# S5 read-out products put off behind the next query product, with banks from the heads' pool, in a hybrid decoder layer in fp32

## The chip, the cores and the metric

The kernel runs on one core of a Trainium2 chip, in one launch. The metric is device time in microseconds (us); the median of three runs stands for a kernel. Five engines work side by side, each through its own list of instructions in order: TensorE (PE, matmuls, with its weight loads as PEld), VectorE (DVE), ScalarE (ACT), GpSimd (POOL) and SyncE (SP, which issues most DMAs).

## The reference, cut to what matters

One layer is computed for 16 meta tokens and 2048 prompt tokens, and for one step of 8 decoding streams. A norm and one input projection feed two mixers. The S5 mixer (A) runs a complex diagonal state over the tokens for 32 groups of 16 channels, reads it out and puts it through gelu and a gate. The HGRN mixer (B) has 4 heads with a 128x128 state each. Both go through an output projection, and then comes a gated ConvFFN.

```python
u, q, fl, iv, g = columns of rms_norm(h) @ w_in
# A: S5
x  = einsum(u, bb)                       # input into 64 complex states a group
h  = associative_scan(a, x)              # h_t = a h_{t-1} + x_t
y  = Re(einsum(h, c)) + d * u
y  = gelu(y);  y5 = y * sigmoid(y @ w_glu + b_glu)
# B: HGRN2, per head, in chunks
f  = lb + (1 - lb) * sigmoid(fl);  k = 1 - f
o  = qd @ S + mask(qd @ kd^T) @ v;  S = f_chunk * S + kd'^T @ v
yh = rms_norm(o) * norm_g * silu(g)
h  = h + concat(y5, yh) @ w_out
h  = h + (silu(conv(a)) * v) @ w_down    # a, v = rms_norm(h) @ w_up
```

## The kernel before

All large products are in fp32, done as three passes on fp32r halves: high by high, low by high, high by low. Activations lie as pairs `ah`, `al`, weights as `wh` (made by ACT, L449) and `wl` (by DVE, L83). Tokens go in four blocks of 512; block 0 also carries the 16 meta tokens and the 8 streams as extra columns.

**Heads.** In each block `head()` runs four times. It makes the forget-gate product f (L480, 24 matmuls of 512 columns), its tanh (L642), the scans and the reciprocal on DVE (L645 to L665), the query product q (L480, 24 more), and the input and gate product i/g (L500, 96 matmuls of 256 columns, in two halves `t2_`). Then comes the attention part: kd by qd (L723) and the transposes of kd (L729) into two banks, the masked copy att (L726), kd by v (L734) into a third bank, the output (L746, L747), its norm and the gate (L756). Its last step, the transposes into feature order (L768), is a closure in the list `PEND`.

**S5.** The S5 work of block b-1 runs in the heads of block b. It has eight table steps `bt` of four groups each. `s5()` takes two steps before each head in blocks 1 and 2. In the last block it takes four steps of block 2 before each of heads 0 and 1; before head 2 it runs the first four steps of the last block itself, between the halves of the output projection of block 2, and two steps before each of heads 2 and 3. A step loads its table (L881, `big`, two buffers), makes the input products Bk (L896, four fp32 matmuls), swaps real and imaginary halves on ACT (L272, L273), multiplies and scans on DVE (L86, L80, L934), swaps and multiplies back (L86, L83) to the state G (`sA`), and then reads out: six products with the direct term (L945) and G (L948) into one bank, which ACT copies to Y (L954). For the S5 work of block 0 six more small products (L960, L963) read out the extra columns. Every second step ends in `s5_finish()`: gelu on DVE with one tanh on ACT (L851 to L856), four transposes of Y (L863; L872 for the extra columns), the high half by ACT (L866) and the low half by DVE (L867). The finish is a closure in `PEND`, too.

**Order.** A scheduler fixes the order of each engine's instructions when the kernel is built; what stands in a row on PE runs in that row. Buffers of a pool are given out in the order of the program, and a tile gets its buffer only when the last user of the one before it is through. PSUM has eight banks in three pools: `bank()` (3, `mm`) for large products, `tbank()` (2, `tp`) for Bk, read-outs and transposes, and `gbank()` (3, `hg`) for the attention banks L723, L729 and L734 and the transposes L768. `flush()` runs what is in `PEND`. It stands in `head()` behind the f product, in `u_proj()` behind each of its four products, in `stage_out()` and at the end of the mixers.

Of the kernel before, what the change touches and what calls it, by code (L numbers as in the profile page):

```python
# [9 lines left out]
F32 = mybir.dt.float32  # L10
F32R = mybir.dt.float32r
U32 = mybir.dt.uint32
AF = mybir.ActivationFunctionType
# [24 lines left out]
def kernel(  # L38
# [468 lines left out]
    def tm_wide(src, c0, lhs, done, ex=None, first=None, rows=None):  # L507


        pb = [(bank, gbank)[t % 2]() for t in range(4)]  # L510
        pe = bank() if ex is not None else None
        for i in range(4):
            wu = first if first is not None and i == 0 else w_unit(src, 2 * i, 2, c0, 512)
            if i == 1:
                rows()
            for t in range(4):
                for kk in range(2):
                    k = 2 * i + kk
                    for j, (wi, ai) in enumerate(PASS):
                        mm(pb[t], lhs(ai, k, t), wu[wi][:, kk, :], start=(k == 0 and j == 0),  # L520
                           stop=(k == 7 and j == 2))
                if i == 3:
                    done(t, pb[t])
            if ex is not None:
                stat, m = ex
                for kk in range(2):
                    for j in range(2):
                        mm(pe[:m], stat[:, 2 * i + kk, :m], wu[j][:, kk, :], start=(i + kk + j == 0),
                           stop=(i == 3 and kk == 1 and j == 1))
        return pe  # L530
# [96 lines left out]
    PEND = []  # L627

    def flush():
        while PEND:  # L630
            PEND.pop(0)()


    def head(b, a, h):
# [8 lines left out]
        flush()  # L643
# [23 lines left out]
        pq = fm_mm(wq, a, 8, cols)  # L667
        qd = P
# [148 lines left out]
    def u_proj(b, a):  # L817
# [60 lines left out]
    def s5(b, ut, m, bts, later=None):  # L878
        for bt in bts:
            tab = bigt()  # L880
# [22 lines left out]
            if b == 0:  # L903
# [4 lines left out]
                mw = sm.tile([128, 4, 4], F32, name="mw", bufs=1)  # L908
# [18 lines left out]
                he = sm.tile([128, 4, 9], F32, name="he", bufs=1)  # L927
# [14 lines left out]
            py = v3(tbank(), 4, 64)  # L942
            o = None
            for i in range(2):
                behind(mm(py[:, 2 * i:2 * i + 2, :].rearrange("p a b -> p (a b)"), UT[:, i, 0:128], T[:, i, :],  # L945
                          start=True, stop=False), o)
                for j in range(2):
                    o = mm(py[:, 2 * i:2 * i + 2, :].rearrange("p a b -> p (a b)"), G[:, 2 * i + j, 0:128],  # L948
                           Cm[:, 2 * i + j, :], start=False, stop=(j == 1))
            half = bt % 2  # L950
            if half == 0:
                Y = E["Y"] = s5p.tile([128, 4, 128], F32, name="sY")
            Y = E["Y"]
            ACT(Y[:, :, 64 * half:64 * half + 64].rearrange("p t (g c) -> p g t c", c=16),  # L954
                py.rearrange("p g (t c) -> p g t c", c=16), AF.Copy)
            if b == 0:
                pye = v3(tbank(), 4, 64)
                o = None
                for i in range(2):
                    behind(mm(pye[:9, 2 * i:2 * i + 2, :].rearrange("p a b -> p (a b)"),  # L960
                              UT[:, i, 131:140], T[:, i, :], start=True, stop=False), o)
                    for j in range(2):
                        o = mm(pye[:9, 2 * i:2 * i + 2, :].rearrange("p a b -> p (a b)"), he[:, 2 * i + j, :],  # L963
                               Cm[:, 2 * i + j, :], start=False, stop=(j == 1))
                if half == 0:
                    E["ye"] = s5p.tile([128, 4, 128], F32, name="sY")
                ye = E["ye"]
                ACT(ye[:9, :, 64 * half:64 * half + 64].rearrange("p t (g c) -> p g t c", c=16),
                    pye[:9].rearrange("p g (t c) -> p g t c", c=16), AF.Copy)
            if half == 1:  # L970
                fin = lambda m, bt=bt, Y=Y, ye=E.get("ye"): s5_finish(b, bt, Y, ye, m)
                if later is None:
                    PEND.append(lambda fin=fin: fin(m))
                else:
                    later.append(fin)
# [173 lines left out]
    flush()  # L1149
# [208 lines left out]
```

## Time and profile before

| | us |
|---|---|
| median of 3 runs | 2537.81 |
| lowest and highest run | 2536.32, 2539.64 |
| the profiled execution | 2535.7 |
| its span in the trace | 2534.0 |
| PE busy in the span | 2445.5 |
| DVE busy in the span | 1453.3 |
| ACT busy in the span | 902.6 |

The trace comes from the profiled execution. Its span leaves out what lies around the program, 1.7 us here. A busy time is the sum of an engine's work over the whole span, so it averages over stages: norms, set-up, tables and block 0 first; then blocks 1 to 3 with the S5 work, whose read-outs (L945) start between 276.7 and 952.1 us; and the FFN, which fills the window from 1060 to 2500 us. A matmul in three passes shows as three rows; an fp32 matmul (L723, L896, L945, L948, L863) shows as two passes, so that a row with x8 holds four of them. Matmul ends overlap the next start.

### The profile page before, as it was taken

The page shows a single profiled execution, that of the slowest core. Times are in us where ns is not written, and L with a number is a line of the kernel's source. Part 1 is how long each engine was busy: PE and PEld are TensorE (multiplying, and loading weights), DVE is VectorE, ACT ScalarE, POOL GpSimd, SP SyncE. Part 2 cuts the span into 40 slices and gives each one's busy share as a digit, 9 for nine tenths or more (in the row PEclk, how much of TensorE's full clock was granted, in tenths as well). Part 3 has the DMA queues.
Part 4 walks back from the last instruction along what each step waited for, and adds up shares of the span by engine and source line. Part 5 has one row for each costly group of instructions (what it writes and reads, how often), then busy time and mean ns, then how long its engine had stood idle before and what let it go on. Part 6 is the DMA issues. An engine that isn't in the chain of part 4 may idle for free.

```text
span 2534.0 us, 33854 instructions
## 1 busy us (share of the span) xinstructions
PE 2445.5 (97%) x13515; PEld 2088.5 (82%) x13515; DVE 1453.3 (57%) x2950; ACT 902.6 (36%) x1548; POOL 166.6 (7%) x252
## 2 busy tenths in 40 slices
PE   7989899999999989999999999999999999999998
PEld 6878787788888778888989898988788888888886
DVE  6897788688678688553343434445843433343344
ACT  3554445344435444432313131323531313131222
POOL 2223001000100001000000000000400000000000
PEclk9999999999999999999999999999999999999999
DMA  4357435543564555531111111111621111111112
GB/s 126 103 159 205 114 101 141 191 142 127 148 215 158 162 164 192 170 92 43 50 44 48 47 45 42 46 55 59 211 66 50 44 48 50 50 50 50 34 54 80
DMA packets 251260, 252.13 MB, mean 99 GB/s; under 512 B 11303, under 2 KB 208751, under 8 KB 246998
## 3 DMA queue, kind: packets, MB, share of 16 engines
q1 hardware_dynamic: 241088, 220.42, 28.8%
q0 software_dynamic: 9840, 29.48, 3.6%
q8 instruction: 106, 1.74, 0.3%
q14 instruction: 52, 0.43, 0.1%
q10 hardware_dynamic: 174, 0.06, 0.0%
HBM read 216.41 MB, written 33.27 MB: 99 GB/s over the span
## 4 chain that ended last, share of the span: by engine, by line
PE 72%; DVE 11%; issue 4%; ACT 3%; DMA 1%; POOL 1%; SPq 0%; POOLq 0%; ACTq 0%; DVEq 0%
PE mm L480 42%; PE mm L1282 9%; PE hg L1282 9%; PE mm L500 3%; PE hg L520 3%; PE mm L520 2%; DVE sB L86 2%; DVE sA L934 1%; DVE wl L83 1%; DVE sA L86 1%; PE mm L539 1%; DVE hf L665 1%; POOL rstd L546 1%; DMA x<-h_d 1%; PE tp L572 1%
## 5 line engine op out<-in xcount | busy, mean ns | idle before, releaser
L480 PE MATMUL mm<-ah,wh 128*128 128x512 f32 (+3 forms) x2312 | 811.6, 351 | 5.9 <-ACT ah L577 3.3
L480 PE MATMUL mm<-al,wh 128*128 128x512 f32 (+3 forms) x2312 | 810.8, 351 | 1.1 <-DVE al L83 1.1
L480 PE MATMUL mm<-ah,wl 128*128 128x512 f32 (+3 forms) x2312 | 810.8, 351 | 1.0 <-DVE wl L83 1.0
L449 ACT ACTIVATE wh<-st 128x1024 fp32r<-128x1024 f32 (+1 forms) x264 | 276.4, 1047 | 709.2 <-PE mm L480 298.0
L83 DVE TENSOR_TENSOR wl<-st,wh 128x1024 fp32r<-128x1024 f32 (+1 forms) x264 | 318.4, 1206 | 350.4 <-ACT wh L449 348.4
L480 PEld LDWEIGHTS mm<-ah,wh 128*128 128x128 f32 x2312 | 438.9, 190 | 59.7 <-ACT ah L577 3.9
L480 PEld LDWEIGHTS mm<-ah,wl 128*128 128x128 f32 x2312 | 438.7, 190 | 56.2 <-issue 1.6
L480 PEld LDWEIGHTS mm<-al,wh 128*128 128x128 f32 x2312 | 438.1, 189 | 54.8 <-DVE al L83 1.6
L86 DVE TENSOR_TENSOR c<-c,mm 128x512 f32<-128x512 f32 (+1 forms) x110 | 63.6, 580 | 211.7 <-PE mm L480 210.3
L500 PE MATMUL mm<-wh,ah 128*128 128x256 f32 x512 | 146.3, 286 | 3.0 <-DVE hP L86 1.7
L500 PE MATMUL mm<-wl,ah 128*128 128x256 f32 x512 | 144.8, 284 | 1.7 <-DVE wl L83 1.7
L500 PE MATMUL mm<-wh,al 128*128 128x256 f32 x512 | 145.9, 285 | 0.0
L1282 PE MATMUL mm<-wh,gh 128*128 128x512 f32 x352 | 137.4, 390 | 0.0
L1282 PE MATMUL hg<-wh,gl 128*128 128x512 f32 x352 | 137.1, 390 | 0.0
L1282 PE MATMUL hg<-wl,gh 128*128 128x512 f32 x352 | 137.1, 390 | 0.0
L1282 PE MATMUL mm<-wh,gl 128*128 128x512 f32 x352 | 137.1, 389 | 0.0
L1282 PE MATMUL mm<-wl,gh 128*128 128x512 f32 x352 | 137.1, 389 | 0.0
L1282 PE MATMUL hg<-wh,gh 128*128 128x512 f32 x352 | 137.0, 389 | 0.0
L80 DVE TENSOR_TENSOR hacc<-hacc,hg 128x512 f32<-128x512 f32 x96 | 65.8, 686 | 88.2 <-PE hg L1282 87.7
L1220 ACT ACTIVATE c<-c 128x512 f32<-128x512 f32 x88 | 55.6, 632 | 144.8 <-DVE c L1219 144.8
L80 DVE TENSOR_TENSOR hacc<-hacc,mm 128x512 f32<-128x512 f32 x96 | 65.7, 685 | 66.0 <-PE mm L1282 65.8
L500 PEld LDWEIGHTS mm<-wh,ah 128*128 128x128 f32 x512 | 97.7, 191 | 4.7 <-DVE hP L86 2.5
(406 smaller groups left out, 3569.0 us busy)
## 6 DMA issues: line engine op xcount, KB each, us to landing
st<-in_ffn_w_up_dram SPq DMA_DIRECT2D x96, 512.0 KB, 3.8
big<-tab_d SPq DMA_DIRECT2D x32, 1156.0 KB, 5.4
st<-in_w_in_dram SPq DMA_DIRECT2D x48, 512.0 KB, 5.0
st<-in_ffn_w_down_dram SPq DMA_DIRECT2D x40, 512.0 KB, 3.5
st<-in_w_in_dram SPq DMA_DIRECT2D x64, 256.0 KB, 3.1
st<-in_w_out_dram SPq DMA_DIRECT2D x32, 512.0 KB, 3.6
x<-in_x_prompt_dram SPq DMA_DIRECT2D x30, 512.0 KB, 5.0
h_d<-x POOLq DMA_DIRECT2D x16, 512.0 KB, 4.2
```

What stands on the lines that cost most here:

```text
L80: tt_(o, a, b, op=OP.add)
L83: tt_(o, a, b, op=OP.subtract)
L86: tt_(o, a, b, op=OP.mult)
L449: ACT(hi[:, :n], st[:, :n], AF.Copy)
L480: mm(p[:, :n], w[wi][:, k, :], a[ai][:, k, c0:c0 + n], start=(i == 0), stop=(i == 3 * nk - 1))
L500: o = mm(dst, lhs(ai, k), (hi, lo)[wi][:, kk, :], start=(i == 0), stop=(i == tot - 1))
L520: mm(pb[t], lhs(ai, k, t), wu[wi][:, kk, :], start=(k == 0 and j == 0), stop=(k == 7 and j == 2))
L539: mm(dst[:m], stat[:, k, :m], w[:, kk, :], start=(i == 0), stop=(i == tot - 1))
L546: nc.gpsimd.tensor_tensor(r, r, mhalf[:ss.shape[0], :n], op=OP.pow)
L572: nc.tensor.transpose(p[:, k, :], x[:, kk * 128:kk * 128 + 128], ident)
L1220: ACT(c, c, AF.Silu)
L1282: mm(ps_[t], gs[b, f0 + k][ai][:, t * 128:t * 128 + 128], wus[i][wi][:, kk, :], start=(k == 0 and j == 0), stop=(k == nf - 1 and j == 2))
```

## The change

The read-out products of a step (L945, L948, and L960, L963 for the extra columns), the copies to Y and the hand-over to `s5_finish` become a closure `products`, put into `PEND`; `s5()` runs the list itself if two closures of its call are waiting. Their banks, and those of the transposes in `s5_finish`, come from `gbank()`. In `head()`, `flush()` moves from behind the tanh of f to behind the q product, and it is called in `tm_wide()` with the second weight tile. The finish goes to a second list, `PEND2`, which `flush2()` runs (after `flush()`) behind each half of the i/g products, behind the products 1 to 3 of `u_proj()`, in `stage_out()` and at the end. Two small tiles of the extra columns change: `mw` gets another shape, `he` a second buffer.

```diff
@@ tm_wide
                 if i == 3:
                     done(t, pb[t])
+            if i == 1:
+                flush()
@@
-    PEND = []
+    PEND, PEND2 = [], []
...
+    def flush2():
+        flush()
+        while PEND2:
+            PEND2.pop(0)()
@@ head
             ACT(f[:, q0:q0 + n], p[:, :n], AF.Tanh, scale=0.5)
-        flush()
...
         pq = fm_mm(wq, a, 8, cols)
+        flush()
...
             ACT(g[:, 2 * t2_:2 * t2_ + 2], p[:, :, 128:256], AF.Silu)
+            flush2()
@@ u_proj
-            flush()
+            (flush if ch == 0 else flush2)()
@@ s5_finish
-        p = v3(tbank(), 4, 128)
+        p = v3(gbank(), 4, 128)
...
-            p = v3(tbank(), 3, 16)
+            p = v3(gbank(), 3, 16)
@@ s5
+        backs = []
         for bt in bts:
+            if len(backs) > 1:
+                flush()
+                backs.clear()
...
-                mw = sm.tile([128, 4, 4], F32, name="mw", bufs=1)
+                mw = v3(sm.tile([128, 40], F32, name="mw", bufs=1), 4, 4)
...
-                he = sm.tile([128, 4, 9], F32, name="he", bufs=1)
+                he = sm.tile([128, 4, 9], F32, name="he", bufs=2)
...
-            py = v3(tbank(), 4, 64)
-            o = None
-            for i in range(2):
...
+            def products(bt=bt, UT=UT, T=T, G=G, Cm=Cm, he=he if b == 0 else None):
+                py = v3(gbank(), 4, 64)
+                o = None
+                for i in range(2):
...
-                pye = v3(tbank(), 4, 64)
...
+                    pye = v3(gbank(), 4, 64)
...
-                    PEND.append(lambda fin=fin: fin(m))
+                        PEND2.append(lambda: fin(m))
...
+            backs.append(products)
+            PEND.append(products)
@@ stage_out
-        flush()
+        flush2()
@@ behind the last block
-    flush()
+    flush2()
```

The rows below are PE's order at two places, first before and then after. In the rows of after the lines have moved: L908 is Bk (L896 before), L959 and L962 are the products (L945, L948), L974 and L977 those of the extra columns, L871 and L880 the transposes (L863, L872), L731 and L737 attention's first two (L723, L729), L742 kd by v (L734), L754 and L755 the output (L746, L747). Names: `hg`, `tp` and `mm` are banks of the three pools, `U` the S5 input, `sA` G, `sY` Y, `big` a table, `hk`, `hP`, `hv`, `hf` the head's kd, qd, v and transposed kd.

On PE in block 1, the end of head 0 before: the last i/g product, attention, and the first f products of head 1.

```order
L500 MATMUL mm<-wl,ah 128x256
L723 MATMUL hg<-hP,hk 128x128 x4
L729 MATMUL hg<-ident,hk 128x128 x4
L746 MATMUL mm<-hv,att 128x128
L747 MATMUL mm<-Sp,hP 128x128
L734 MATMUL hg<-hv,hf 128x128 x4
L746 MATMUL mm<-hv,att 128x128
L480 MATMUL mm<-ah,wh 128x512
```

Thirty rows on in the same list, amid the f products of head 1, stand head 0's transposes and the first S5 work of the block.

```order
L480 MATMUL mm<-ah,wl 128x512
L768 MATMUL hg<-ident,hg 128x128 x4
L896 MATMUL tp<-U,big 128x148 x4
L480 MATMUL mm<-ah,wh 128x512
L480 MATMUL mm<-al,wh 128x512
L945 MATMUL tp<-big,U 128x128
L500 MATMUL mm<-wh,ah 128x256
```

The same place after, from the last products of the pair's second step on; the Bk products of both steps and the other products stand directly ahead of these rows, and ahead of those the last i/g product of head 0.

```order
L962 MATMUL hg<-big,sA 128x128 x2
L959 MATMUL hg<-big,U 128x128
L962 MATMUL hg<-big,sA 128x128 x2
L908 MATMUL tp<-U,big 128x148 x4
L871 MATMUL hg<-ident,sY 128x128 x4
L880 MATMUL hg<-ident,sY 128x9 x3
L731 MATMUL hg<-hP,hk 128x128 x4
L737 MATMUL hg<-ident,hk 128x128 x4
L908 MATMUL tp<-U,big 128x148 x3
L742 MATMUL hg<-hv,hf 128x128 x4
L754 MATMUL mm<-hv,att 128x128
L755 MATMUL mm<-Sp,hP 128x128
```

The first pair's Bk products, products and transposes have moved from amid head 1's products to between head 0's i/g products and its attention.

On PE in the last block, the end of head 1 before: the last i/g products, attention, a Bk product, and a read-out.

```order
L500 MATMUL mm<-wh,al 128x256
L500 MATMUL mm<-wl,ah 128x256
L723 MATMUL hg<-hP,hk 128x128 x4
L729 MATMUL hg<-ident,hk 128x128 x4
L896 MATMUL tp<-U,big 128x128 x4
L734 MATMUL hg<-hv,hf 128x128 x4
L746 MATMUL mm<-hv,att 128x128
L747 MATMUL mm<-Sp,hP 128x128
L948 MATMUL tp<-big,sA 128x128 x2
L945 MATMUL tp<-big,U 128x128
L948 MATMUL tp<-big,sA 128x128 x2
```

Further on in the list of before, amid the L480 of the projection that follows, stand the last but one transposes and the last read-out (the last transposes come 26 rows behind these).

```order
L480 MATMUL mm<-al,wh 128x512
L863 MATMUL tp<-ident,sY 128x128 x4
L948 MATMUL tp<-big,sA 128x128 x2
L945 MATMUL tp<-big,U 128x128
L948 MATMUL tp<-big,sA 128x128 x2
L480 MATMUL mm<-ah,wl 128x512
```

The end of head 1 after.

```order
L500 MATMUL mm<-wl,ah 128x256
L871 MATMUL hg<-ident,sY 128x128 x4
L962 MATMUL hg<-big,sA 128x128 x2
L959 MATMUL hg<-big,U 128x128
L962 MATMUL hg<-big,sA 128x128 x2
L871 MATMUL hg<-ident,sY 128x128 x4
L731 MATMUL hg<-hP,hk 128x128 x4
L737 MATMUL hg<-ident,hk 128x128 x4
L754 MATMUL mm<-hv,att 128x128
L755 MATMUL mm<-Sp,hP 128x128
L742 MATMUL hg<-hv,hf 128x128 x4
L754 MATMUL mm<-hv,att 128x128
```

Both sets of transposes and the last read-out now stand between the i/g products and attention, the second set directly behind that read-out.

## Rows read from the trace of the kernel before

**Rows 1.** The page: the span, two engines’ busy time, and the chain by engine.
```profile
span 2534.0 us, 33854 instructions
...
PE 2445.5 (97%) x13515; PEld 2088.5 (82%) x13515; DVE 1453.3 (57%) x2950; ACT 902.6 (36%) x1548; POOL 166.6 (7%) x252
...
PE 72%; DVE 11%; issue 4%; ACT 3%; DMA 1%; POOL 1%; SPq 0%; POOLq 0%; ACTq 0%; DVEq 0%
```

**Rows 2.** Windows: length, then each engine’s busy us, granted clock, DMA share, GB/s.
```profile
core 0: us, PE busy (x) PEld busy (x) DVE busy (x) ACT busy (x) POOL busy (x), PEclk, DMA share, GB/s
259.00:427.00 168.00, 154.63 (x969) 126.99 (x968) 136.47 (x398) 81.75 (x200) 9.51 (x13) 0.98 0.36 113
497.00:631.00 134.00, 128.91 (x877) 115.10 (x876) 118.86 (x249) 60.22 (x114) 6.25 (x8) 1.00 0.45 144
717.00:760.80 43.80, 41.58 (x280) 36.35 (x279) 42.67 (x87) 20.81 (x34) 0.73 (x1) 1.00 0.61 203
760.80:810.00 49.20, 47.11 (x312) 41.64 (x312) 45.69 (x100) 26.18 (x54) 4.11 (x6) 1.00 0.48 157
850.00:965.00 115.00, 103.05 (x636) 87.60 (x635) 97.66 (x192) 51.23 (x84) 6.65 (x10) 1.00 0.49 160
1060.00:2500.00 1440.00, 1438.58 (x7277) 1223.64 (x7276) 616.00 (x1050) 402.83 (x571) 33.02 (x54) 1.00 0.19 58
```

**Rows 3.** PE’s waits: who was waited for, us in total, times, longest.
```profile
PE tp L948 <- DVE sA L83: 5.2, 12, 1.0
PE tp L945 <- DVE sB L86: 4.0, 7, 1.1
PE tp L945 <- ACT pe L906: 3.7, 5, 2.3
PE tp L945 <- DVE al L867: 3.3, 2, 2.6
```

**Rows 4.** Timeline of PE, last block, heads 0 and 1: start, duration, operation.
```profile
749.77 0.49 PE L723 MATMUL hg<-hP,hk 128*128 128x128 f32 x3
...
760.25 0.66 PE L863 MATMUL tp<-ident,sY 128*128 128x128 f32 x4
...
789.43 1.16 PE L723 MATMUL hg<-hP,hk 128*128 128x128 f32 x8
...
809.59 0.66 PE L863 MATMUL tp<-ident,sY 128*128 128x128 f32 x4
```

**Rows 5.** Timeline of PE, block 1: heads’ attention, first S5 matmul, last transposes.
```profile
259.05 1.05 PE L723 MATMUL hg<-hP,hk 128*128 128x128 f32 x8
...
270.17 1.25 PE L896 MATMUL tp<-U,big 128*128 128x148 f32 x8 [0.25 <-issue]
...
305.58 1.05 PE L723 MATMUL hg<-hP,hk 128*128 128x128 f32 x8
306.47 0.60 PE L729 MATMUL hg<-ident,hk 128*128 128x128 f32 x4
...
345.87 1.05 PE L723 MATMUL hg<-hP,hk 128*128 128x128 f32 x8
...
385.81 1.05 PE L723 MATMUL hg<-hP,hk 128*128 128x128 f32 x8
...
426.45 0.66 PE L863 MATMUL tp<-ident,sY 128*128 128x128 f32 x4
```

**Rows 6.** Timeline of DVE, block 1: a step’s first and last large operation.
```profile
293.97 0.42 DVE L86 TENSOR_TENSOR sB<-tp,big 128x256 f32<-128x256 f32 x1 [2.30 <-ACT sA L273]
...
303.13 0.70 DVE L83 TENSOR_TENSOR sA<-sA,sB 128x516 f32<-128x516 f32 x1
```

**Rows 7.** Timeline of PE, last block, head 3: a read-out’s first product.
```profile
905.71 0.49 PE L945 MATMUL tp<-big,U 128*128 128x128 f32 x2 [2.59 <-DVE al L867]
```

**Rows 8.** The page’s DMA issues: the table load, KB each, us to landing.
```profile
big<-tab_d SPq DMA_DIRECT2D x32, 1156.0 KB, 5.4
```

More of the change, by code (lines that the diff above doesn't have):

```diff
@@ L941, in s5 @@
             nc.vector.tensor_copy(Hc[:, 4 * bt:4 * bt + 4], G[:, :, 128])
-            py = v3(tbank(), 4, 64)
-            o = None
-            for i in range(2):
[L945 to L956, printed above, removed]
-                pye = v3(tbank(), 4, 64)
+            def products(bt=bt, UT=UT, T=T, G=G, Cm=Cm, he=he if b == 0 else None):
+                py = v3(gbank(), 4, 64)
@@ L958, in s5 @@
                 o = None
                 for i in range(2):
-                    behind(mm(pye[:9, 2 * i:2 * i + 2, :].rearrange("p a b -> p (a b)"),
-                              UT[:, i, 131:140], T[:, i, :], start=True, stop=False), o)
+                    behind(mm(py[:, 2 * i:2 * i + 2, :].rearrange("p a b -> p (a b)"), UT[:, i, 0:128], T[:, i, :],
+                              start=True, stop=False), o)
                     for j in range(2):
-                        o = mm(pye[:9, 2 * i:2 * i + 2, :].rearrange("p a b -> p (a b)"), he[:, 2 * i + j, :],
+                        o = mm(py[:, 2 * i:2 * i + 2, :].rearrange("p a b -> p (a b)"), G[:, 2 * i + j, 0:128],
@@ L964, in s5 @@
                                Cm[:, 2 * i + j, :], start=False, stop=(j == 1))
+                half = bt % 2
                 if half == 0:
[L966 to L972, printed above, removed]
-                    PEND.append(lambda fin=fin: fin(m))
-                else:
-                    later.append(fin)
+                    Y = E["Y"] = s5p.tile([128, 4, 128], F32, name="sY")
@@ new lines, in products @@
+                Y = E["Y"]
+                ACT(Y[:, :, 64 * half:64 * half + 64].rearrange("p t (g c) -> p g t c", c=16),
+                    py.rearrange("p g (t c) -> p g t c", c=16), AF.Copy)
+                if b == 0:
+                    pye = v3(gbank(), 4, 64)
+                    o = None
+                    for i in range(2):
+                        behind(mm(pye[:9, 2 * i:2 * i + 2, :].rearrange("p a b -> p (a b)"),
+                                  UT[:, i, 131:140], T[:, i, :], start=True, stop=False), o)
+                        for j in range(2):
+                            o = mm(pye[:9, 2 * i:2 * i + 2, :].rearrange("p a b -> p (a b)"), he[:, 2 * i + j, :],
+                                   Cm[:, 2 * i + j, :], start=False, stop=(j == 1))
+                    if half == 0:
+                        E["ye"] = s5p.tile([128, 4, 128], F32, name="sY")
+                    ye = E["ye"]
+                    ACT(ye[:9, :, 64 * half:64 * half + 64].rearrange("p t (g c) -> p g t c", c=16),
+                        pye[:9].rearrange("p g (t c) -> p g t c", c=16), AF.Copy)
@@ L976, in s5 @@
+                if half == 1:
+                    fin = lambda m, bt=bt, Y=Y, ye=E.get("ye"): s5_finish(b, bt, Y, ye, m)
+                    if later is None:
+                        PEND2.append(lambda: fin(m))
+                    else:
+                        later.append(fin)
+            backs.append(products)
+            PEND.append(products)
         if bts[-1] != 7:
```

## The prediction

> **What bounds the kernel now.** I read the page first. PE is busy 97% of the span and carries 72% of the chain that ended last; DVE is busy 57% on average [rows 1]. With 88.5 us of PE idle in 2534, and with the same PE instructions in both kernels, only idle time of PE can change the total. Next I read busy time by stage [rows 2]. From 1060 us on PE is busy 1438.58 of 1440 us: nothing that the change touches runs there, and a delay that reaches it is not given back. The stages that hold S5 work are the first five windows. In each PE has a few idle us, but DVE differs: 81% in block 1 (259 to 427), 89% in block 2 (497 to 631), and in the last block's heads 0 and 1, which carry four table steps each, 42.67 of 43.80 and 45.69 of 49.20 us. In those two heads DVE is full, and the average of 57% hides it.
>
> Third I read who PE waits for [rows 3]. The waits that this change aims at are the first product of a read-out (L945), which waits for a t-pool bank to be released by sB, pe or al (4.0 + 3.7 + 3.3 us), and the second (L948), which waits for its data G (5.2 us): 16.2 us in all. Last I read where in time the products, transposes and attention stand [rows 4 to 7].
>
> **The change part by part.** PE runs the same matmuls, DVE and ACT the same operations; so every term is a change of waiting. No DMA is added. The closures issue none; but a table buffer (two of them) is free only after its step's products, so table loads come later. They take 5.4 us to land [rows 8], and after the products stand the 96 i/g matmuls before the next pair's Bk products, so I count nothing; where that cover is missing (four steps per head, the third Bk some twenty L480 behind the products) it costs up to 1 us a step. The mw and he tiles and the moved flush calls add no instruction. POOL's and SP's rows keep their work.
>
> *Last block, heads 0 and 1.* Before, the attention of head 0 (L723) starts at 749.77 and the second gelu's transposes run at 760.25, amid the next head's L480; for head 1 it is 789.43 against 809.59 [rows 4]. The banks of the heads' pool are given in the order of the program, so the transposes now stand ahead of the head's L723, and right behind the products that they wait for. PE then cannot start L723 of head 1 before DVE has done the work that it finished, before, just ahead of 809.59. DVE has 4.6 us of idle time in these 93 us [rows 2], so that work ends between 805.0 and 809.6. L723 starts 16.2 to 20.8 us later than 789.43 (0.6 us for the transposes included at either end). Some of the PE work that ran between these two points is then already behind PE: four Bk products, two sets of six products, two sets of transposes, 24 fp32 matmuls at 0.22 us each (eight passes of L723 take the 0.89 us from 305.58 to 306.47 [rows 5]), so 5.4 us. The delay is 10.8 to 15.4 us. As Bk products of steps 4 to 7 stand somewhat earlier now, DVE may begin sooner; for that I let the range go down to 8, and take 11.5, near the end at which DVE uses its gaps. Behind it u_proj is PE work alone, and nothing gives it back.
>
> Every matmul behind a waiting transpose waits with it: at 905.71 L945 waited 2.59 us for a bank, and no L480 ran in that gap [rows 7]. The Trainium skill, TensorE: Matmul & The Clock Gate, "Step-by-step: what each phase is for", says the same as a rule: only weight loads are pulled ahead, matmuls stay in program order. By that rule the forward move of a transpose in PE's order is a cost wherever its data are late, and the trace agrees.
>
> *Block 1, head 0.* Before, L723 stood at 259.05 and the first S5 matmul at 270.17, amid head 1's L480 [rows 5]. Now the Bk products, both steps' products and the gelu's transposes stand between head 0's i/g products and its L723, with no L480 among them. From the first x product on DVE (293.97) to G at the end of L83 (303.83) takes 9.9 us [rows 6] with little else on DVE. So: Bk 1.25, swap 0.8 (an estimate from the 2.30 us that DVE waited for it), 9.9 for the first G, about 7 for the second, whose operations overlap the first's waits, about 5 for Y, tanh and two gelus: 25 us of chain, and L723 at about 284 rather than 259. What comes back: by then a pair of steps is done, 43 fp32 matmuls or 9.5 us that no longer stand behind L723 of head 3; and the heads that follow don't have the first pair's stall (46.5 us from 259.05 to 305.58). The last gap between heads was 39.9 us (345.87 to 385.81). Three heads at 38 us, and a tail from L723 of head 3 of 40.6 (385.81 to 426.45) less 9.5 and some 3 of its waits, give 25 + 114 + 28 = 167 us, against 167.4 from 259.05 to 426.45. At 36 us a head (what DVE's work of a head allows: 136.47 over some four heads, with gaps) it is 6 us better, at 40 6 us worse. PE's clock may fall in the hole, which is 16 us (25 less 9.5): the window's granted clock was 0.98 of 2.4 GHz [rows 2], so stretches at the lower clock cost it 3.4 us. I take +1, from -6 to +8.
>
> *Block 2.* Both steps' products come behind the q product. The second one stands where it stood, the first moves back, so bank waits of L945 go, and L948 waits for DVE instead: the second G, then gelu, transposes, attention. PE idles 5.1 us there in all [rows 2]. I take -1, from -4 (nearly all of it) to +1.
>
> *850 to 965.* PE idles 12 us here. The 2.59 us wait [rows 7] goes, since no t-pool bank is held by a gelu; but the products of the last steps and their transposes stand ahead of the head's L723, some 7 us of PE work earlier, while their G is behind the reciprocal of the head on DVE, which is busy 97.66 of 115. I take +2, from -4 (the bank waits of L945 here gone, nothing new) to +6.
>
> Sum: 11.5 + 1 - 1 + 2 = +13.5 us. The profiled execution took 2535.7, so 2549.2; the median of the runs lies 2.1 above it, so about 2550 to 2551. I say 2550. The likeliest case's own range is 2541 to 2561 (the terms' ends combined, not all at one side).
>
> **Rivals.**
> Faster: the waits of the read-out were the idle time, and they go. The price is L945's 11.0 us and L948's 5.2 [rows 3]: 2537.8 - 16.2 = about 2522. For it: al, pe and sB release a bank, all three things with which a product has nothing to do. Against it: where PE waits longest DVE is full, and a product that need not wait for a bank then waits for G. It decides if the last G and gelu of a pair end before the head's i/g products do; DVE at 93 to 97% in the heads with four steps speaks against that, DVE at 81% in block 1 for it.
> The Trainium skill, Perfetto Trace Analysis, "Identifying Performance Opportunities", reads repeated gaps of the engine that should be full as a lack of PSUM or SBUF buffers. By that rule this rival is the forecast. The trace bears it out for the 11.0 us at L945 only.
> No change: the loop of a head (DVE, Y, gelu, transposes, attention, state) sets the time in both kernels, PE's holes only move, and the last block's heads lose what block 1's later heads gain at 36 us each: 2535 to 2542. For it: the same work, and DVE within 11% of full in block 2. Against it: the L480 that covered the last gelu in the last block are behind it now.
> Much slower: block 1's heads, coupled to DVE by L723, take 40 us each, and the clock falls after every hole: +6 + 3.4 there, 15 in the last block, 6 behind it: 2537.8 + 29 = about 2567. For it: no L480 stands beside the waiting products. Against it: DVE has 31 us of idle time in block 1.
> That the change doesn't do what it says: the order shows that it does, except that block 1's first pair is ahead of attention rather than amid the i/g products. That is in the sum.
>
> **How the numbers follow.** Forecast 0.55, much slower 0.13, no change 0.17, faster 0.15. What a measurement of this kernel tells from no change is about 0.2%, 5 us. Faster by more than that: the faster rival and a hundredth of the forecast (the terms' low ends add to -6 us), 0.16. Within it: 0.17. Slower: 0.67. The range takes in no change, the weak end of the faster rival and the lower half of much slower, and leaves out 0.11 below and 0.07 above: 2531 to 2564.
>
> **What would show it right or wrong.** Right: in the last block L723 of head 1 starts 16 us or more after 789, directly behind the gelu's transposes, with DVE over 90% busy up to it, and u_proj ends 10 us or more later. In block 1, PE has a hole of some 15 us between the last i/g product of head 0 and its L723, and the following heads come every 36 to 40 us. L945's waits for sB, pe and al are gone, L948's or the transposes' waits for DVE are longer. From the second normalisation on PE is as full as before. Wrong: if PE's idle time in the last block's two heads is no more than its 4.3 us now, or if L723 of head 1 starts within 5 us of 789; or if block 1 ends more than 8 us before or after 427.

## The result, and the profile after

The changed kernel takes 2568.77 us (median of 4 runs, 2568.47 to 2570.93) against 2538.72 us before; the ratio is 1.0121, with a 95% interval of 1.0105 to 1.0137. It is 30 us slower. The forecast was 2550 with a range up to 2564: the direction was right and the size was not. The two traces lie 35.2 us apart, as the profiled execution after is the slowest of its four (2570.93) and the one before (2535.7) is below all four of its runs; so the losses by stage below add up to 5 us more than the medians show.

Rows of the changed kernel carry the moved line numbers that are listed with the change; L864, where gelu ends (L856 before), is one more.

First the page of the changed kernel: span, busy time, and the chain that ended last.

```profile
span 2569.2 us, 33852 instructions
...
PE 2451.3 (95%) x13515; PEld 2108.8 (82%) x13515; DVE 1455.2 (57%) x2950; ACT 901.0 (35%) x1548; POOL 167.2 (7%) x252
...
PE 73%; DVE 9%; issue 4%; ACT 3%; DMA 3%; POOL 1%; POOLq 0%; SPq 0%; DVEq 0%; ACTq 0%
```

The span grew by 35.2 us [rows 1] and PE's busy time by 6 only: the rest is PE waiting. To see where, take a point that every kernel has, the first matmul of each block's output projection (L520), and read its start from the timelines. Before it is at 440.9, 669.6, 833.4 and 982.3 us, with the end at 2534.0; after it is at 453.0, 685.2, 866.5 and 1019.2, with the end at 2569.2. So block 1 with all that comes ahead of it lost 12.1 us, block 2 3.5, the last block's heads 0 and 1 (with u_proj behind them) 17.5, its second part 3.8, and the FFN gave 1.7 back.

The windows of the same stages after (length, busy us of PE, PEld, DVE, ACT, POOL, then PE's granted clock, DMA share, GB/s):

```profile
259.00:440.00 181.00, 157.59 (x978) 136.81 (x978) 136.99 (x403) 81.92 (x201) 9.63 (x13) 0.91 0.36 112
509.00:646.00 137.00, 127.85 (x873) 118.60 (x872) 117.49 (x248) 59.61 (x113) 6.22 (x8) 0.98 0.42 140
732.50:779.20 46.70, 37.25 (x242) 33.96 (x241) 44.12 (x88) 21.63 (x35) 0.72 (x1) 0.88 0.62 203
779.20:827.30 48.10, 39.58 (x265) 35.33 (x265) 41.37 (x88) 21.68 (x41) 2.50 (x3) 0.96 0.40 137
883.00:1002.00 119.00, 104.82 (x635) 91.62 (x634) 98.43 (x192) 51.30 (x83) 6.33 (x10) 0.96 0.47 154
1100.00:2540.00 1440.00, 1439.69 (x7269) 1223.74 (x7268) 612.59 (x1041) 401.73 (x571) 32.78 (x54) 1.00 0.19 58
```

Each answers to a window of [rows 2]. In the last block's two heads (third and fourth row) PE was busy 88.7 of 93.0 us before and is busy 76.8 of 94.8 now, and DVE, which was full with 88.4 us, has 85.5 us of work: the engine that was to set the pace now has holes too. The granted clock fell in every stage with S5 work, to 0.91 in block 1 and 0.88 in head 0 of the last block. The FFN's window is as full as before.

PE's waits after (who was waited for, us in all, times, longest), against [rows 3]:

```profile
PE hg L962 <- DVE sA L83: 16.7, 13, 3.0
PE hg L871 <- DVE sY L864: 15.6, 8, 5.2
PE tp L908 <- DMA big<-tab_d: 10.3, 4, 4.4
...
PE tp L908 <- DMA U<-udx: 4.7, 1, 4.7
```

The waits for sB, pe and al at the first product are gone, as the change intends: 11.0 us. But products and transposes now wait 16.7 + 15.6 us for DVE, and Bk 10.3 us for tables. In [rows 3] products waited 16.2 us in all, banks included. The like sum of 16.7 us now is not the same wait put elsewhere: between the output projections of blocks 1 and 2 the products waited 4.4 us before and wait 8.0 us now, and in the last block they wait less than before. The products' waits in that stretch, before (440.9 to 669.6 us) and after (453.0 to 685.2):

```profile
PE tp L948 <- DVE sA L83: 2.3, 4, 0.6
PE tp L945 <- DVE sB L86: 2.1, 4, 0.7
```

```profile
PE hg L962 <- DVE sA L83: 8.0, 4, 2.3
```

The wait for gelu came on top. Of the 10.3 us for tables, 3.8 lie in the last block's heads 0 and 1 and 6.5 in its second part (2.10 us at 909.88, 4.41 at 949.71).

Timeline of PE in block 1 behind head 0's i/g products, after; it answers to the first two rows of [rows 5]:

```profile
264.43 2.31 PE L908 MATMUL tp<-U,big 128*128 128x148 f32 x8 [4.72 <-DMA U<-udx]
...
280.82 1.22 PE L962 MATMUL hg<-big,sA 128*128 128x128 f32 x4 [2.98 <-DVE sA L83]
...
294.18 1.12 PE L871 MATMUL hg<-ident,sY 128*128 128x128 f32 x4 [3.26 <-DVE sY L864]
295.23 0.48 PE L880 MATMUL hg<-ident,sY 9*128 9x9 f32 x3
295.64 2.08 PE L731 MATMUL hg<-hP,hk 128*128 128x128 f32 x8
```

L731 starts at 295.64, 36.6 us later than before [rows 5]. Bk first waits 4.72 us for the U columns; then the pair's chain takes 31.2 us with nothing but small S5 products on PE. The eight passes of L731 take 2.08 us (1.05 before [rows 5]): this is the lower of the clock's two levels.

DVE's timeline in the same hole: the first step's first product with a table, the last operation of its G and of the second step's G, and gelu's first.

```profile
266.59 0.42 DVE L86 TENSOR_TENSOR sB<-tp,big 128x256 f32<-128x256 f32 x1 [8.23 <-ACT sA L273]
...
280.07 0.69 DVE L83 TENSOR_TENSOR sA<-sA,sB 128x516 f32<-128x516 f32 x1
...
285.48 0.69 DVE L83 TENSOR_TENSOR sA<-sA,sB 128x516 f32<-128x516 f32 x1
...
290.18 1.28 DVE L86 TENSOR_TENSOR sB<-sY 128x512 f32<-128x512 f32 x2 [3.81 <-ACT sY L968]
```

The first G takes 14.2 us, the second 5.4 more, and from there to the transposes it is 8.0. Ahead of the first G DVE also made two weight halves (2.45 us) and did the second step's first operations.

Timeline of PE in the last block, heads 0 and 1, after, against [rows 4]:

```profile
768.72 1.19 PE L908 MATMUL tp<-U,big 128*128 128x128 f32 x4 [3.08 <-DMA big<-tab_d]
...
778.29 1.11 PE L871 MATMUL hg<-ident,sY 128*128 128x128 f32 x4 [4.54 <-DVE sY L864]
779.20 1.91 PE L731 MATMUL hg<-hP,hk 128*128 128x128 f32 x8
...
826.41 1.12 PE L871 MATMUL hg<-ident,sY 128*128 128x128 f32 x4 [5.23 <-DVE sY L864]
827.32 1.91 PE L731 MATMUL hg<-hP,hk 128*128 128x128 f32 x8
```

In both heads PE waits 4.5 to 5.2 us for the last gelu, does its transposes, and only then starts attention. L731 of head 1 now comes 94.8 us after the start of this stage's window (732.5); before it was 72.4 (789.43 less 717.0).

### The profile page after: what moved, and what is told of

It reads as the page before. It is cut to its first block, busy times and chain, and to the rows that moved or that the text cites. A ratio compares the mean times of both kernels' runs of the same rounds, so it can differ in the third digit from the quotient of the medians.

```text
span 2569.2 us, 33852 instructions
## 1 busy us (share of the span) xinstructions
PE 2451.3 (95%) x13515; PEld 2108.8 (82%) x13515; DVE 1455.2 (57%) x2950; ACT 901.0 (35%) x1548; POOL 167.2 (7%) x252
## 4 chain that ended last, share of the span: by engine, by line
PE 73%; DVE 9%; issue 4%; ACT 3%; DMA 3%; POOL 1%; POOLq 0%; SPq 0%; DVEq 0%; ACTq 0%
PE mm L480 40%; PE mm L1299 9%; PE hg L1299 9%; PE mm L500 3%; PE hg L520 3%; PE mm L520 3%; DVE sA L946 1%; DVE wl L83 1%; DVE sB L86 1%; POOL rstd L548 1%; PE mm L541 1%; DVE hf L671 1%; PE tp L908 1%; DVE sA L86 1%; PE hg L962 1%
## 5 line engine op out<-in xcount | busy, mean ns | idle before, releaser
L480 PE MATMUL mm<-ah,wh 128*128 128x512 f32 (+3 forms) x2312 | 808.2, 350 | 3.7 <-ACT ah L579 3.3
L480 PE MATMUL mm<-al,wh 128*128 128x512 f32 (+3 forms) x2312 | 808.0, 350 | 1.1 <-DVE al L83 1.1
L480 PE MATMUL mm<-ah,wl 128*128 128x512 f32 (+3 forms) x2312 | 807.0, 349 | 0.0
L480 PEld LDWEIGHTS mm<-ah,wh 128*128 128x128 f32 x2312 | 437.5, 189 | 58.3 <-ACT ah L579 3.9
L480 PEld LDWEIGHTS mm<-ah,wl 128*128 128x128 f32 x2312 | 437.6, 189 | 55.1 <-issue 0.9
L480 PEld LDWEIGHTS mm<-al,wh 128*128 128x128 f32 x2312 | 437.1, 189 | 54.7 <-DVE al L83 1.6
L86 DVE TENSOR_TENSOR c<-c,mm 128x512 f32<-128x512 f32 (+1 forms) x110 | 63.6, 579 | 211.6 <-PE mm L480 210.3
```

Of the source, the lines that this page charges most:

```text
L86: tt_(o, a, b, op=OP.mult)
L480: mm(p[:, :n], w[wi][:, k, :], a[ai][:, k, c0:c0 + n], start=(i == 0), stop=(i == 3 * nk - 1))
```

## The experiments

Two theories and a side one were set against each other. P: the pool. The heads' banks are asked for in the order of the program, so attention's bank stands behind those of the S5 read-out. D: the deferral. Products put off hold the tables, Bk comes late and DVE starves. C: TensorE's clock after the holes. Medians and ratios are against the kernel before on the same chip; the stage columns are one profile each, as above (us lost against before).

| kernel | median us | ratio, interval | block 1 | block 2 | heads 0, 1 | second part |
|---|---|---|---|---|---|---|
| changed | 2568.77 | 1.0121, 1.0105 to 1.0137 | 12.1 | 3.5 | 17.5 | 3.8 |
| e1_banks | 2567.64 | 1.0114, 1.0096 to 1.0131 | 18.9 | 1.3 | 15.0 | -2.6 |
| e2_defer | 2549.27 | 1.0046, 1.0031 to 1.0061 | 6.3 | 2.4 | 7.8 | -3.0 |
| e3_fin_t | 2561.36 | 1.0096, 1.0077 to 1.0116 | 10.6 | 3.6 | 9.1 | 3.5 |
| e4_fin_late | 2588.45 | 1.0196, 1.0179 to 1.0212 | 17.8 | 0.4 | 20.3 | 11.3 |
| e6_four_now | 2574.5 | 1.0131, 1.0112 to 1.015 | 21.1 | 3.5 | 17.4 | 1.6 |
| e9_fin_g | 2579.87 | 1.0159, 1.0138 to 1.0181 | 34.7 | -0.3 | 12.2 | 0.6 |
| e10_two_only | 2542.8 | 1.0023, 1.0013 to 1.0032 | 10.3 | 2.4 | 0.0 | -2.5 |
| e11_behind_att | 2566.03 | 1.0112, 1.009 to 1.0133 | 8.8 | 3.1 | 9.5 | 9.3 |
| e12_pt3 | 2542.74 | 1.0012, 1.0 to 1.0024 | -2.9 | 1.6 | 7.5 | 1.8 |
| e14_b1_shift | 2556.57 | 1.0074, 1.0061 to 1.0088 | -1.5 | 3.5 | 16.1 | 2.4 |
| e15_filler | 2574.7 | 1.0148, 1.0134 to 1.0162 | 13.4 | 2.5 | 18.7 | 5.6 |
| e16_part2 | 2533.76 | 0.9982, 0.9973 to 0.9991 | 1.2 | -0.1 | 0.0 | -3.2 |

Block 1's column spreads: the changed kernel, e6_four_now and e15_filler have the same order there but for the filler and lose 12.1, 21.1 and 13.4 us, as their first Bk starts at 264.43, 273.41 and 267.82. Much of this spread comes from ahead of that S5 work, where the three programs do not differ: head 0's last i/g product starts at 259.42, 267.19 and 260.82 in them, and at 258.93 before. Counted from that product they lose 11.6, 12.8 and 11.5 us, e1_banks 12.6, e9_fin_g 26.4, e2_defer 3.6, e10_two_only 5.9, and e14_b1_shift gains 3.6. As the column stands, differences under some 9 us show nothing. In the other three columns the changed kernel, e14_b1_shift and e15_filler, which do not differ there, spread by 1.0, 2.6 and 3.2 us.

**e1_banks**, the kernel before with the banks alone:

```diff
-            py = v3(tbank(), 4, 64)
+            py = v3(gbank(), 4, 64)
-                pye = v3(tbank(), 4, 64)
+                pye = v3(gbank(), 4, 64)
# s5_finish
-        p = v3(tbank(), 4, 128)
+        p = v3(gbank(), 4, 128)
-            p = v3(tbank(), 3, 16)
+            p = v3(gbank(), 3, 16)
```

> The kernel before with one part of the change alone: the banks of the read-out products and of the gated transposes come from the heads' pool, at the old places of the program. Theory P (the pool: attention's banks are given out behind those of the products and transposes, so L723 waits for S5): L723 of block 1's head 0 again stands behind the S5 chain (some 296 us against 259), and both sets of transposes precede L723 in the last block; 2555 to 2568 us. Theory D (the deferral: products put off hold the tables, Bk comes late and DVE starves): with no deferral the time is that of before, 2535 to 2545. Theory C (TensorE's clock after holes in block 1 makes most of it): as P in block 1 alone, 2548 to 2553.

Measured: 1.0114, a loss as large as the whole change's without any deferral. P holds; D as the only cause falls. PE's timeline in block 1 shows the same picture as the changed kernel's (here with the line numbers of before; `st`, named in the first row, is not read by Bk, whose last U columns land at 271.38 in this trace):

```profile
272.00 2.31 PE L896 MATMUL tp<-U,big 128*128 128x148 f32 x8 [6.54 <-DMA st<-in_w_in_dram]
...
301.46 0.66 PE L863 MATMUL hg<-ident,sY 128*128 128x128 f32 x4 [2.90 <-DVE sY L856]
302.16 0.32 PE L872 MATMUL hg<-ident,sY 9*128 9x9 f32 x3
302.41 2.08 PE L723 MATMUL hg<-hP,hk 128*128 128x128 f32 x8
```

**e2_defer**, the changed kernel with those four banks from `tbank()`:

```diff
-                py = v3(gbank(), 4, 64)
+                py = v3(tbank(), 4, 64)
-                    pye = v3(gbank(), 4, 64)
+                    pye = v3(tbank(), 4, 64)
# s5_finish: both banks from tbank() likewise
```

> The changed kernel with the deferral, the two lists and the new flush places kept, but all banks of products and transposes from the t pool as before. Theory P: L723 is free again, so block 1 and the last block's heads come back to before, and only the later tables cost: 2536 to 2548 us. Theory D: the table waits (10.3 us in the changed kernel, 2.4 before) and the late Bk stay, 2555 to 2570. Theory C: 2540 to 2550, as the clock stays high where attention fills the hole.

Measured: 1.0046, 1 us above P's range, inside C's and well below D's; with the hole gone this run can't tell C from P. L731 of block 1's head 0 is back at its place:

```profile
261.70 1.05 PE L731 MATMUL hg<-hP,hk 128*128 128x128 f32 x8
```

What is left is 12.6 us, the largest part in the last block's heads (7.8): the deferral has a price of its own there.

**e3_fin_t**, the changed kernel with only the transposes' banks from `tbank()`:

```diff
# s5_finish
-        p = v3(gbank(), 4, 128)
+        p = v3(tbank(), 4, 128)
-            p = v3(gbank(), 3, 16)
+            p = v3(tbank(), 3, 16)
```

> The changed kernel with only the gated transposes' banks back in the t pool; the read-out products keep the heads' pool. L723 of a head then stands behind the products of its block's pair but not behind gelu. Theory P: block 1's head 0 still waits for both G's (L723 near 288 rather than 296 us), the last block's two heads lose 5 us rather than 17: 2546 to 2556 us. Theory D: no change against the changed kernel within 5 us, 2564 to 2572.

Measured: 1.0096, 5 us above P's range, below D's. The first of L731's four matmuls comes behind the first step's products, the other three (292.81) behind the second step's, and gelu's transposes come behind attention (298.05):

```profile
290.15 0.80 PE L731 MATMUL hg<-hP,hk 128*128 128x128 f32 x2
```

The last block's heads lose 9.1 us instead of 17.5, more than the 5 expected; e2_defer loses 7.8 there with no product bank in the heads' pool, so the products' banks cost little in these heads, and the transposes' banks and the deferral make the loss. In the second part it is the other way round: 3.5 here against -3.0.

**e4_fin_late**, the changed kernel with gelu and transposes put off to the next head:

```diff
# head, behind the tanh of f
+        while PEND2:
+            PEND2.pop(0)()
# head, behind each half of i/g
-            flush2()
```

> The changed kernel with the gelu and its transposes put off to the place behind the tanh of the next head's f product (before's place for them), banks from the heads' pool. L723 is then ahead of its own head's gelu, but the read-outs of two more steps stand ahead of it. Theory P: the 3 to 5 us waits of the last transposes directly ahead of L723 go, the wait for G stays: 2550 to 2562 us. Theory D: 2562 to 2575, tables are held as long. If it is the gelu amid the i/g products alone that hurts, it falls to 2538 to 2545.

Measured: 1.0196, slower than either theory's numbers and the worst of all. It refutes that the gelu amid the i/g products alone is at fault. The waits of the transposes, which were to go, doubled from 15.6 to 31.0 us (L872 and L865 in this file are L871 and L864 of the changed kernel):

```profile
PE hg L872 <- DVE sY L865: 31.0, 10, 7.8
```

Why each stage of the 52 us came about was not followed further.

**e6_four_now**, the changed kernel without the deferral in the calls of four steps:

```diff
+            if len(bts) == 4:
+                products()
+                continue
             backs.append(products)
             PEND.append(products)
```

> The changed kernel without the deferral in the calls of four steps (last block, heads 0 and 1, and the four steps between the halves of the output projection are single calls and stay): products run at once there, with banks from the heads' pool. Theory P (attention's bank is asked for behind the products' and transposes' banks, L723 waits for S5): both sets of transposes still precede L723; the stretch of these two heads stays some 15 us longer than before; 2563 to 2571. Theory D (products put off hold the tables): the stretch comes back by 10 to 17 us, 2551 to 2559.

Measured: 1.0131, and 17.4 us in the two heads against 17.5. As long as the pool puts transposes ahead of attention, undoing the deferral there brings nothing. P's number was missed by 3.5 us at the top; in this trace head 0's last i/g product of block 1 already stands 7.8 us later than in the changed kernel's.

**e9_fin_g**, the kernel before with only the transposes' banks from the heads' pool:

```diff
# s5_finish
-        p = v3(tbank(), 4, 128)
+        p = v3(gbank(), 4, 128)
-            p = v3(tbank(), 3, 16)
+            p = v3(gbank(), 3, 16)
```

> The kernel before with one thing changed: the gated transposes (not the read-out products) take their banks from the heads' pool, at their old place in the program, behind the tanh of the next head. Theory P: PE's order puts the transposes of head 0 of block 1 ahead of its L723 and both sets ahead of L723 in the last block, as in the changed kernel, so the time is 2555 to 2570 although no product's bank has moved. If the read-out products' banks are what hurts: 2536 to 2545.

Measured: 1.0159, above P's range: the banks of the transposes alone cost 41 us (in this trace 8.3 us of it stand ahead of block 1's S5 work). PE's timeline in the last block (line numbers of before) has both waits of the changed kernel:

```profile
793.69 1.11 PE L863 MATMUL hg<-ident,sY 128*128 128x128 f32 x4 [3.53 <-DVE sY L856]
794.60 1.91 PE L723 MATMUL hg<-hP,hk 128*128 128x128 f32 x8
...
839.59 1.12 PE L863 MATMUL hg<-ident,sY 128*128 128x128 f32 x4 [5.30 <-DVE sY L856]
840.50 1.92 PE L723 MATMUL hg<-hP,hk 128*128 128x128 f32 x8
```

In block 1 its products, too, stand ahead of L723 (310.92), since the transposes cannot run before them.

**e10_two_only**, e2_defer with products at once in the calls of four steps:

```diff
+            if len(bts) == 4:
+                products()
+                continue
             backs.append(products)
```

> The kernel of run e2_defer (deferral and new flush places, all banks from the t pool) with products at once in the calls of four steps. Theory D for what was left there (tables held by products put off, so Bk late): the 7.8 us that it lost in the last block's heads 0 and 1 go, 2538 to 2544. If the gelu amid the i/g products is what costs there: no change, 2547 to 2552.

Measured: 1.0023, and 0.0 us lost in the two heads against 7.8: there the deferral, and not the gelu's place, was the rest. PE's waits for tables in these heads are none in this trace and 4.2 us in that of e2_defer. So pool and deferral each cost in these heads (15.0 for the banks alone in e1_banks, 12.2 for the transposes' alone in e9_fin_g, 7.8 for the deferral alone, 17.5 together), and they overlap: e6_four_now has the banks without the deferral and loses 17.4.

**e11_behind_att**, the changed kernel with both lists run behind the head's kd by v:

```diff
# head
         pq = fm_mm(wq, a, 8, cols)
-        flush()
# behind each half of i/g
-            flush2()
# behind kv
+        flush2()
```

> The changed kernel with the same banks from the heads' pool and the same two lists, but both lists are run behind the head's product kd by v, so that attention asks for its three banks first. Theory P: L723 of block 1's head 0 is back at 259 to 262 us and ahead of the transposes in the last block; 2538 to 2552, though the products hold the tables longer than in any other kernel. Theory D: the tables come later still, so slower than the changed kernel, 2570 to 2590.

Measured: 1.0112. Neither range holds: P's order came about (attention of head 0 at 261.3), but not P's time. PE's waits say why (in this file L729 is attention's first product, L907 is Bk):

```profile
PE hg L729 <- DVE hk L86: 18.2, 6, 11.1
PE tp L907 <- DMA big<-tab_d: 10.3, 8, 2.6
```

Attention now waits up to 11.1 us for its own kd (`hk`, made by L86 on DVE). At that longest wait (940.54, last block, head 2) DVE works on S5 up to 931 us and on the head's scans, more S5 work and the reciprocal up to 940; and PE's order has L729 behind only the first four rows of the head's i/g products, with the rest behind it. Giving attention its bank first is not enough; the orders that the scheduler then gives DVE and PE couple the two chains as well.

**e12_pt3**, the kernel before with another split of the banks:

```diff
-    pt = pool("pt", 2, space=PSUM)
+    pt = pool("pt", 3, space=PSUM)
-    pg = pool("pg", 3, space=PSUM)
+    pg = pool("pg", 2, space=PSUM)
```

> The kernel before with eight PSUM banks split 3 + 3 + 2 rather than 3 + 2 + 3: a third bank for the t pool, one fewer for the heads. It takes away what L945 waits for in the kernel before (11.0 us) without putting L723 behind S5 in block 1. If those bank waits were time: 2525 to 2534. If they only move to the wait for G: 2534 to 2541. If two banks are too few for attention or for the FFN's two halves: over 2545.

Measured: 1.0012, 2542.74: between the expected cases, no gain. PE's waits at the read-out:

```profile
PE tp L948 <- DVE sA L83: 12.4, 18, 1.5
...
PE tp L945 <- DVE sB L86: 0.5, 1, 0.5
...
PE tp L945 <- DVE al L83: 0.3, 1, 0.3
```

The bank waits of [rows 3] at L945 fell from 11.0 to under 1 us, and the wait for G rose from 5.2 to 12.4; 3.9 us of waiting for `pe` now stand at L960 and 2.4 for `al` at L896. The Trainium skill, Perfetto Trace Analysis, "Identifying Performance Opportunities", says that a gap which repeats on the engine that should be full can mean that there is not enough SBUF or PSUM for the next tile; here one more bank in the pool in question made no gain, and DVE's G was next in line. That the bank waits were no time at all is not shown: the bank came from the heads, the last block's heads 0 and 1 lose 7.5 us in the profile, and this may hide a small gain in block 1 (-2.9).

**e14_b1_shift**, the changed kernel with block 1's pairs behind the heads:

```diff
-            elif b > 0:
+            elif b > 1:
                 s5(b - 1, U[b - 1], M[b - 1], (2 * h, 2 * h + 1))
             MIX[b].append(head(b, A[b], h))
+            if b == 1:
+                s5(0, U[0], M[0], (2 * h, 2 * h + 1))
```

> The changed kernel with one call moved: in block 1 the pair of S5 steps of head h is called behind head h, not ahead of it, so head 0's attention asks for its bank before any S5 does. Theory P: L723 of head 0 of block 1 is back at 259 to 262 us, the hole of some 36 us goes, block 1 ends 8 to 14 us earlier (the last pair then runs beside the projection that follows); 2554 to 2562. If the hole is not what costs, and block 1 is bound by DVE with the hole given back by the heads behind it: within 4 us of the changed kernel, 2565 to 2572.

Measured: 1.0074, 2556.57, as P expected. L731 of head 0 in the timeline:

```profile
261.17 1.05 PE L731 MATMUL hg<-hP,hk 128*128 128x128 f32 x8
```

Block 1 now ends 1.5 us ahead of before; its whole loss came from the pairs' place ahead of attention, the first pair's above all. The other stages stay as in the changed kernel.

**e15_filler**, the changed kernel with 32 more matmuls in the hole:

```diff
+                if b == 0 and bt == 0:
+                    for _ in range(32):
+                        mm(py[:, 0:2, :]..., UT[:, 0, 0:128], T[:, 0, :], start=True, stop=True)
```

> The changed kernel with 32 more matmuls on TensorE in the hole of block 1's head 0: the first product of the first step repeated into its own bank, where the real one then overwrites them (the result does not change). They run while PE waits for G, and should keep TensorE's clock from staying at half. Theory C (clock): products, transposes and attention behind them run at full clock, L723 comes 3 to 7 us earlier and so does the end: 2562 to 2566. If the chain on DVE and ACT alone sets the hole: 2567 to 2570. If they delay the products: over 2571.

Measured: 1.0148; the number falls in the last case, but the products were not delayed (the first product with G starts 15.7 us behind Bk, 16.4 without the filler). The windows from the first Bk to L731, of the changed kernel and then of this one:

```profile
264.40:295.60 31.20, 19.29 (x79) 14.61 (x79) 20.88 (x67) 14.30 (x37) 0.00 (x0) 0.55 0.33 110
```

```profile
267.80:297.50 29.70, 22.25 (x143) 19.61 (x143) 21.47 (x68) 14.22 (x37) 0.00 (x0) 0.79 0.34 116
```

The granted clock in the hole rose from 0.55 to 0.79, and the stretch became 1.5 us shorter, not 3 to 7: DVE and ACT set most of it. C falls as the main cause of block 1's loss; what the lower clock costs behind the hole, where it was down again, this run doesn't test. Bk started 3.4 us later in this profile, but block 1 ended only 1.3 us later; why the span is 3.6 us longer and the runs lose 6 us is open.

**e16_part2**, the kernel before with e1_banks' banks in the last block's own S5 work alone:

```diff
-            py = v3(tbank(), 4, 64)
+            py = v3((gbank if b == NB - 1 else tbank)(), 4, 64)
# s5_finish
-        p = v3(tbank(), 4, 128)
+        p = v3((gbank if b == NB - 1 else tbank)(), 4, 128)
```

> The kernel before with banks from the heads' pool for products and transposes in the S5 work of the last block alone, where run e1_banks was 2.6 us faster than before between 833 and 982 us. Meant as a version that might beat both kernels: 2532 to 2538 if that gain is real, 2538 to 2542 if it was given back behind that stretch.

Measured: 2533.76, ratio 0.9982 with an interval of 0.9973 to 0.9991: faster than the kernel before by some 4 us. The windows from the output projection of block 2 to that of the last block, before and here:

```profile
833.40:982.30 148.90, 135.22 (x793) 114.26 (x793) 117.00 (x229) 65.21 (x112) 9.30 (x14) 1.00 0.48 155
```

```profile
834.50:980.20 145.70, 135.63 (x793) 117.18 (x792) 118.49 (x229) 65.17 (x112) 9.01 (x14) 0.98 0.49 158
```

PE does the same 793 matmuls in 145.7 instead of 148.9 us. Here the heads carry two steps, and half of the read-outs stand beside the output projection, with no attention to hold up; that this is the reason is not shown.

No run has a third table buffer, which would tell the tables' share directly.

## Why the prediction was wrong

- **The direction, and that nothing is given back** behind 1060 us, were right: the end moved by 35.2 us where the last stage had left 36.9.
- **Block 1: the term failed** (+1 forecast, from -6 to +8; +12.1 measured), and with it came a sign that was named for being wrong, block 1's end more than 8 us late. The place was right, the chain ahead of L723. Two sizes were not. The chain was set at 25 us, with L723 at 284; it came at 295.64. 5.4 us of this is Bk, which I let start with the end of the i/g products: its U columns were not there before 264.43, a wait that the L480 of head 1 covered before, and I had not asked what covers the moved instruction's data. 6 us more is the chain itself, 31.2 us from Bk to L731: the first G took 14.2 us where I had read 9.9 with little else on DVE, the second 5.4 instead of 7, and Y to the end of gelu 8.0 instead of 5. The heads behind it took 39.3 us each (295.64 to 413.5 for three), not 38. The tail, from head 3's attention to the projection, is 39.5 us against 55.1, better than I gave it. 36.6 late, less 8.9 from three heads (117.9 against 126.8), less 15.6, is the 12.1. e14_b1_shift shows that the pairs' place is the cause; e15_filler that the clock in the hole is 1.5 us of it at the 0.79 that was reached.
- **Last block, heads 0 and 1: right mechanism, mis-sized** (+11.5, from 8 to 15; 17.5 measured). The step "DVE uses its gaps" failed. Attention of head 1 came 22.4 us later against its stage's start, where I had 16.2 to 20.8. The work already done is 4.8 us rather than 5.4 (from L723 to the projection it was 44.0 us and is 39.2; a transpose L863 is one row in the trace, not two as the fp32 products), which leaves some 17.5. DVE did not fill its 4.6 us of gaps, it got 9.3 us of them (85.5 busy of 94.8). Its own waits there name ACT: 2.5 us for the high half behind the transposes (1.0 before) and 2.3 for a swap (0.2 before). I had counted nothing for the later table loads; PE's table waits in these heads went from none to 3.8 us (3.08 at 768.72). How much of DVE's gaps the tables made is not shown. e9_fin_g and e2_defer with e10_two_only show both parts, 12.2 for the transposes' banks and 7.8 for the deferral, which overlap.
- **Block 2** (-1, from -4 to +1; +3.5 measured): wrong sign, small. The heads' attention comes every 36.0 us (538.08 to 646.18 for three) instead of 34.7 (526.65 to 630.81). The step that failed is the size of the wait for G, which I took for smaller than the bank waits that go: 2.1 us of these went, and the wait for G rose from 2.3 us to 8.0, 1.2 to 2.3 us in every head. It is 7.6 us in e2_defer, with the banks in the t pool, and 6.5 in e1_banks, without the deferral, so no run takes the two apart.
- **850 to 965** (+2, from -4 to +6; 3.8 measured): held. But e1_banks, e2_defer and e16_part2 are 2.6 to 3.2 us faster than before there, so each half of the change gains in this part and both together lose. With both, 6.5 us of table waits stand there (2.4 before).
- **The faster rival** fell: the bank waits went, waits for G grew, and the changed kernel got no time back. **The much slower rival** had the right total, about 29 us, with a chance of 0.13. Its 40 us a head was close (39.3), but the total is in part luck: its clock price is not borne out in block 1 (e15_filler), and block 2, which it left out, lost 3.5. In the last block, where the granted clock was 0.88 and 0.96, the clock's share was not tested; PE's busy time in the whole trace rose by 5.8 us.

## What to carry to other kernels

A PSUM pool that two chains share ties them together in the order of their requests: before a bank is moved, ask which chain's next request then stands behind the other's slowest operation. A wait for a bank is worth only what the next wait in line leaves; another split of the banks, as in e12_pt3, is a cheap test of that, as long as the pool that gives the bank can spare it. For every instruction that moves forward in an engine's list, ask when its data land, the DMA ones too, and what covered that before.

## What the runs showed of the hardware

PE's timeline in e15_filler (in this file L960 is the repeated product):

```profile
269.93 1.91 PE L960 MATMUL hg<-big,U 128*128 128x128 f32 x8
...
273.15 1.05 PE L960 MATMUL hg<-big,U 128*128 128x128 f32 x8
...
274.62 5.52 PE L960 MATMUL hg<-big,U 128*128 128x128 f32 x48
...
291.47 2.34 PE L908 MATMUL tp<-U,big 128*128 128x148 f32 x8 [1.02 <-DMA big<-tab_d]
...
297.51 2.07 PE L731 MATMUL hg<-hP,hk 128*128 128x128 f32 x8
```

The first eight passes of the repeated product took 1.91 us, the next eight 1.05, and the 48 behind them 5.52: work that only filled the hole brought PE's clock from its lower to its upper level. By the Bk at 291.47 it was down again (2.34 us for eight passes, as in the hole's first Bk), behind waits for G of 1.31 and 2.12 us, and eight passes of L731 took 2.07 us at the hole's end, as without the filler (2.08). Filling the front of a hole did not help what stands behind its end.
